# Down stages of an encoder trunk: where the per layer input is loaded, and how the first result is turned

## The chip, the cores and the metric

The kernel runs on one core of a Trainium2 chip. The metric is the device time of one execution in microseconds (us), as the median over runs. The engines are named as the profile names them: PE (TensorE, matrix products; PEld is its loading of stationary operands), DVE (VectorE), ACT (ScalarE), POOL (GpSimd) and SP (SyncE, which here only issues DMAs). Each engine carries out its own instructions in the order in which they were placed in its program; engines wait for one another through semaphores.

## The reference

An encoder trunk of two layers over one sequence of 512 positions with 1024 features, in float32. What matters here:

```python
for i in range(DEPTH):                       # 2 layers
    h = h + 0.5 * swiglu(rmsnorm(h, norm_ffn1[i]), ffn1_w_gate[i], ffn1_w_up[i], ffn1_w_down[i])
    hn = rmsnorm(h, norm_mix[i])
    h = h + (ab_mixer(hn, ...) if i % 2 == 0 else c_mixer(hn, ...))
    h = h + 0.5 * swiglu(rmsnorm(h, norm_ffn2[i]), ffn2_w_gate[i], ffn2_w_up[i], ffn2_w_down[i])
    gate = jax.nn.sigmoid(rmsnorm(h, norm_ple[i]) @ w_ple_gate[i])
    h = h + gate * (p[i] @ w_ple_proj[i])    # p[i]: 512 x 256, the per layer input
return rmsnorm(h, norm_final)

def swiglu(x, w_gate, w_up, w_down):         # 1024 -> 2816 -> 1024
    return (jax.nn.silu(x @ w_gate) * (x @ w_up)) @ w_down
```

There are four `swiglu` in all, two per layer. The product with `w_down` (2816 x 1024) is the down stage that this document is about. The per layer input `p[i]` is used only behind the second `swiglu` of a layer.

## The kernel before

**Arithmetic.** Every float32 operand of a product is split in two: a high part, which ACT rounds (L154), and a low part, the rest, which DVE subtracts (L155, or L218 where a gain is multiplied in). A product is three matmuls: high by high, low by high, high by low. So each weight block costs ACT one pass, DVE one pass, and PE three.

**The down stage** (`down`, L493) computes a 2816 x 1024 by 2816 x 512 product by blocks with seven products instead of eight: weights and inner activations are cut in quarters, and sums of quarters are multiplied ("first" to "seventh"). Each of the seven runs over eleven pairs of inner chunks, cut into six units of 1, 2, 2, 2, 2 and 2 pairs. That makes 42 steps, and their order on PE is a list written by hand (`order`, L604 to L608): step 10 is fifth 2, step 14 is seventh 0, step 17 fifth 4, step 18 seventh 1, step 24 fourth 0, step 28 sixth 3, step 29 seventh 5, and the last ones are third 3, third 4 and third 5 (39 to 41). A step of unit 0 has six matmuls, any other step twelve.

Three things happen around each step (loop at L689): `product` issues its matmuls (L595); `after` (L640) does what is due behind certain steps; `ahead` prepares the operands of the step four further on (`prepare`, L549: splits, sums of weight blocks on DVE at L566, accumulating loads on POOL at L547) and issues the load of the step seven further on (`load`, L529: a wide block through `wide`, L518 and L520, into one of five `wr` buffers, or narrow blocks through `narrow`, L523 and L526, each into one of ten `tmp` buffers). One `wr` buffer serves several products in turn: its weights are split for one product, another quarter is added to it by an accumulating load, and it is split again. It comes free for the next wide load when its last split is done.

**Order.** What passes through `put` (L150) while `pinned` is set keeps its place in the order of the program on its engine. Everything else is placed by a scheduler, by priority and by when it is ready. In the loop `pinned` is set (L680), so the matmuls, splits and weight loads are in fixed order on PE, ACT, DVE, POOL and SP. The loads of the stored `h` (L658) are not pinned.

**The ends of the stage.** The first result is in `c11` and `c21` after fourth 5; its blocks of 128 features are turned back with PE transposes against an identity (`turned`, L614, four per block), added to `h` by DVE (L625) and split for the next phase (`norm_split`, L217 and L218, not pinned). `first_half(m)` does this for block m of 0 to 3; `second_half` does it for two blocks at a time from 4 to 7 (L635), in halves. The transposes write to one of two PSUM banks (`tbank`), which DVE empties. The last part needs the end of third 5 and a subtraction (L696).

**The per layer input.** In the second `swiglu` of a layer `down` gets a function `inner`. Behind step fourth 0 it calls `per_layer` for each of two chunks: a DMA of 256 KB on SP (L481, not pinned) into a `tmp` buffer, and the split of that buffer on ACT and DVE (L154 and L155, pinned).

Of the kernel before, what the change touches and what calls it, by code (L numbers as in the profile page):

```python
# [56 lines left out]
class Trunk:  # L57
# [92 lines left out]
    def put(self, ins):  # L150
        return self.tc.keep_in_program_order(ins) if self.pinned else ins
# [302 lines left out]
    def ffn(self, i, which, k_next):  # L454


        nc, io = self.nc, self.io
        gu, dn = io[f"gu{which}"][i], io[f"dn{which}"][i]
        first = i == 0 and which == 1
        kept = io["xT"].rearrange("p c t -> c p t") if first else self.put_away()  # L460
        a, sums = [], [None] * K2
        rows, t = self.front(gu, first)
        y = self.xg

        def between():
            a.extend(self.turn_back(rows, self.tbank))
            for k in range(READY):
                if 2 * k + 2 <= len(a) and sums[k] is None:
                    sums[k] = self.inner_sums(*a[2 * k:2 * k + 2])

        for j in range(BLOCKS):
            n = 4 * UNIT + j * 8 * UNIT
            rows = self.block(gu[:, n:n + 8 * UNIT], y, t, between, first and j == 0)
        self.begin_norm(k_next)
        p = lambda: [self.per_layer(i, c) for c in range(2)]
        self.down(dn, a, sums, kept, p if which == 2 else None, lambda n: a.extend(self.turn_back(rows, self.tbank, n)))

    def per_layer(self, i, c):

        raw = self.tmp()  # L480
        self.nc.sync.dma_start(raw, self.io["pT"][i, :, c, :])  # L481
        return self.split_chunk(raw, self.nc.vector)

    def inner_sums(self, a, b):

# [7 lines left out]
    def down(self, w, a, sums, kept, inner, turn):  # L493

        nc, H = self.nc, T // 2
# [6 lines left out]
        n = len(units)  # L502
        r1, r2, r3 = [self.bank(), self.bank()], [self.bank(), self.obank()], [self.sbank(), self.sbank()]
        rb = rc = c11 = c5 = c2 = u3 = c21 = None
        x1, x2, x3, x4, raws, more, ops = ({} for _ in range(7))
        put = self.put
# [91 lines left out]
        def copied(p):  # L598
            out = [self.act() for _ in p]
            for o, x in zip(out, p):  # L600
                put(copy(o, x, AF.Copy))
            return out
# [9 lines left out]
        def turned(out, x, j):  # L612
            for i, y in enumerate(x):
                put(nc.tensor.transpose(out[:, i * P:(i + 1) * P], y[:, j * P:(j + 1) * P], self.ident))  # L614

        def floating(f, *x):
            pinned, self.pinned = self.pinned, False
            f(*x)
            self.pinned = pinned

        def first_half(m):
            p, h = self.tbank(), hs[m]
            turned(p[:, l], c11, m)
            turned(p[:, r], c21, m)
            put(nc.vector.scalar_tensor_tensor(h, p, 0.5, h, op0=ALU.mult, op1=ALU.add))  # L625
            self.h[m] = h
            floating(self.norm_split, m)

        def second_half(m, x, c):
            p = self.tbank()  # L630
            for j in range(2):
                turned(p[:, j * H:(j + 1) * H], x, m - M + j)
            for j in range(2):
                h = hs[m + j]
                put(nc.vector.scalar_tensor_tensor(h[:, c], p[:, j * H:(j + 1) * H], 0.5, h[:, c], op0=ALU.mult, op1=ALU.add))  # L635
                self.h[m + j] = h
            for j in range(2):
                floating(self.norm_split, m + j, c)

        def after(kind, s):  # L640
            nonlocal rb, rc, c11, c5, c2, u3, c21
            if (kind, s) in (("first", 2), ("fifth", 1)):
                turn(range(2) if kind == "first" else range(2, 4))
                if kind == "fifth":
                    rb = [self.tbank(), self.tbank()]
            elif (kind, s) == ("first", 5):
                c11 = copied(r1)
                for o, p in zip(c11, r2):
                    put(tt(o, p, o, op=ALU.add))
                rc = [self.bank(), self.obank()]  # L650
            elif (kind, s) == ("fifth", 5):
                c5 = copied(r3)
            elif (kind, s) == ("fourth", 0) and inner:
                self.p = inner()
            elif (kind, s) == ("first", 3):
                hs.extend(self.act() for _ in range(KC))
                for m in range(KC):
                    nc.sync.dma_start(hs[m], kept[m])  # L658
            elif (kind, s) == ("sixth", 5):
                c2, u3 = copied(r1), [self.act(), self.act()]  # L660
                for i in range(2):
                    put(tt(u3[i], c2[i], rb[i], op=sub))
                for i in range(2):
                    put(tt(c5[i], c5[i], u3[i], op=sub))
            elif (kind, s) == ("fourth", 5):
                c21 = [self.act(), self.act()]
                for i in range(2):
                    put(tt(c21[i], rc[i], u3[i], op=ALU.add))
                second_half(M + 2, c5, r)
            elif (kind, s) == ("third", 2):  # L670
                second_half(M, c5, r)
            elif kind == "third" and 2 < s < 5:
                first_half(2 * s - 6)
                first_half(2 * s - 5)

        for i, step in enumerate(order[:LOADS]):
            load(*step)
# [11 lines left out]
        for i, step in enumerate(order):  # L689
            product(*step)  # L690
            after(*step)
            ahead(i + LEAD + 1)
# [941 lines left out]
```

## Time and profile before

| | us |
|---|---|
| runs | 2001.15, 2001.87, 2005.03 |
| median | 2001.87 |
| the profiled execution | 2003.01 |
| its span (first to last instruction) | 2001.2 |

The first and last matmul of the four down stages, as the trace has them:

| stage | layer, swiglu | loads p | L595 from | to | us |
|---|---|---|---|---|---|
| D1 | 0, first | no | 229.1 | 342.3 | 113.2 |
| D2 | 0, second | yes | 857.1 | 975.1 | 118.0 |
| D3 | 1, first | no | 1252.0 | 1364.8 | 112.8 |
| D4 | 1, second | yes | 1815.3 | 1933.3 | 118.0 |

How to read the rows of the profile. A row of the order of time has the start in us from the start of the span, the duration, the engine, the line of the kernel, the operation, "written<-read" by the names of the buffers, the shape, the count if several were merged, and in brackets the idle time of that engine just before with what ended it. A row of the waits is "engine buffer line <- what it waited for: us in total, times, the longest". A row of a stretch has the stretch, its length, then for PE, PEld, DVE, ACT and POOL the busy time and the count, then the granted TensorE clock as a share of full speed, the share of time for which the DMA engines were busy, and the GB/s that they moved. "SPq" is SP's queue of DMA issues; its rows are the issues, and "DMA to landing" is the time from the issue until the data has arrived.

### The profile page before, as it was taken

The page shows a single profiled execution, that of the slowest core. Times are in us where ns is not written, and L with a number is a line of the kernel's source. Part 1 is how long each engine was busy: PE and PEld are TensorE (multiplying, and loading weights), DVE is VectorE, ACT ScalarE, POOL GpSimd, SP SyncE. Part 2 cuts the span into 40 slices and gives each one's busy share as a digit, 9 for nine tenths or more (in the row PEclk, how much of TensorE's full clock was granted, in tenths as well). Part 3 has the DMA queues.
Part 4 walks back from the last instruction along what each step waited for, and adds up shares of the span by engine and source line. Part 5 has one row for each costly group of instructions (what it writes and reads, how often), then busy time and mean ns, then how long its engine had stood idle before and what let it go on. Part 6 is the DMA issues. An engine that isn't in the chain of part 4 may idle for free.

```text
span 2001.2 us, 28069 instructions
## 1 busy us (share of the span) xinstructions
PE 1974.6 (99%) x9702; PEld 1644.8 (82%) x9702; DVE 1551.5 (78%) x2716; ACT 1218.5 (61%) x2107; POOL 334.7 (17%) x390
## 2 busy tenths in 40 slices
PE   9999999999999999999999999999999999999998
PEld 7888887879888888887888888888888888888786
DVE  8787888698767677787786778887888768678785
ACT  7555656477645555565565556655766556657553
POOL 1111111341211212011122120111000122111111
PEclk9999999999999999999999999999999999999999
DMA  9877697543426777779468785894343577768961
GB/s 275 195 200 163 182 232 229 131 96 80 101 64 226 174 179 183 173 213 252 150 219 184 175 193 153 216 247 150 103 133 101 179 189 189 170 147 229 251 194 42
DMA packets 152223, 348.24 MB, mean 174 GB/s; under 512 B 26512, under 2 KB 34192, under 8 KB 152080
## 3 DMA queue, kind: packets, MB, share of 16 engines
q1 hardware_dynamic: 112128, 235.23, 35.4%
q0 software_dynamic: 39808, 111.17, 31.3%
q8 instruction: 76, 1.25, 0.2%
q14 instruction: 67, 0.55, 0.1%
q10 hardware_dynamic: 144, 0.04, 0.0%
HBM read 318.06 MB, written 17.27 MB: 168 GB/s over the span
## 4 chain that ended last, share of the span: by engine, by line
PE 60%; issue 6%; DVE 6%; DMA 5%; ACT 2%; POOL 1%; SPq 0%; DVEq 0%; POOLq 0%; ACTq 0%
PE mm L179 5%; PE mm L181 5%; PE mm L180 5%; PE mm L595 5%; PE mm L369 4%; PE mm L370 4%; PE mm L368 4%; PE sc L595 3%; DMA wr<-in_gu_dram 3%; PE sc L370 2%; PE sc L369 2%; PE sc L368 2%; DVE wl L155 2%; PE ob L595 2%; PE sc L181 1%
## 5 line engine op out<-in xcount | busy, mean ns | idle before, releaser
L154 ACT ACTIVATE wh<-wr 128x1024 fp32r<-128x1024 f32 (+1 forms) x428 | 438.4, 1029 | 412.1 <-PE mm L370 87.3
L155 DVE TENSOR_TENSOR wl<-wr,wh 128x1024 fp32r<-128x1024 f32 (+1 forms) x428 | 509.8, 1195 | 176.5 <-ACT wh L154 168.0
L368 PE MATMUL mm<-wh,act 128*128 128x512 f32 x640 | 251.0, 392 | 0.0
L370 PE MATMUL mm<-wh,act 128*128 128x512 f32 x640 | 250.8, 392 | 0.0
L369 PE MATMUL mm<-wl,act 128*128 128x512 f32 x640 | 249.5, 390 | 0.1
L179 PE MATMUL mm<-act,wh 128*128 128x512 f32 (+1 forms) x472 | 185.0, 394 | 0.4 <-ACT act L154 0.4
L181 PE MATMUL mm<-act,wl 128*128 128x512 f32 (+1 forms) x472 | 184.6, 392 | 0.0
L180 PE MATMUL mm<-act,wh 128*128 128x512 f32 (+1 forms) x472 | 183.9, 390 | 0.0
L154 ACT ACTIVATE wh<-tmp 128x512 fp32r<-128x512 f32 x248 | 144.9, 623 | 63.8 <-PE sc L370 32.7
L595 PE MATMUL mm<-wh,act 128*128 128x512 f32 x528 | 159.5, 397 | 6.3 <-ACT wh L154 6.3
L155 DVE TENSOR_TENSOR wl<-tmp,wh 128x512 fp32r<-128x512 f32 x248 | 160.5, 684 | 2.9 <-ACT wh L154 2.5
L155 DVE TENSOR_TENSOR act<-act,act 128x512 fp32r<-128x512 f32 (+1 forms) x268 | 141.2, 554 | 3.9 <-ACT act L154 3.7
L338 POOL DMA_DIRECT2D wr<-in_gu_dram x80 | 79.5, 996 | 376.9 <-DVE wl L155 373.4
L369 PEld LDWEIGHTS mm<-wl,act 128*128 128x128 f32 x640 | 120.2, 188 | 24.9 <-DVE wl L155 0.7
L370 PEld LDWEIGHTS mm<-wh,act 128*128 128x128 f32 x640 | 120.2, 188 | 24.4
L368 PEld LDWEIGHTS mm<-wh,act 128*128 128x128 f32 x640 | 120.3, 188 | 23.8
L154 ACT ACTIVATE act<-act 128x512 fp32r<-128x512 f32 (+1 forms) x268 | 125.8, 513 | 15.0 <-DVE act L312 8.3
L368 PE MATMUL sc<-wh,act 128*128 128x512 f32 x320 | 124.7, 390 | 0.5 <-DVE act L292 0.5
L370 PE MATMUL sc<-wh,act 128*128 128x512 f32 x320 | 124.7, 390 | 0.0
L369 PE MATMUL sc<-wl,act 128*128 128x512 f32 x320 | 124.6, 389 | 0.0
L595 PEld LDWEIGHTS mm<-wh,act 128*128 128x128 f32 x528 | 100.3, 190 | 27.9 <-ACT wh L154 7.2
L547 POOL DMA_DIRECT2D wr<-in_dn_dram x72 | 62.3, 880 | 358.4 <-DVE wl L155 352.8
(260 smaller groups left out, 4316.3 us busy)
## 6 DMA issues: line engine op xcount, KB each, us to landing
wr<-in_gu_dram SPq DMA_DIRECT2D x92, 512.0 KB, 4.9
tmp<-in_gu_dram SPq DMA_DIRECT2D x160, 256.0 KB, 3.6
wr<-in_gu_dram POOLq DMA_DIRECT2D x80, 512.0 KB, 7.7
tmp<-in_dn_dram SPq DMA_DIRECT2D x132, 256.0 KB, 6.1
wr<-in_dn_dram POOLq DMA_DIRECT2D x60, 512.0 KB, 7.6
tmp<-in_gu_dram POOLq DMA_DIRECT2D x80, 256.0 KB, 6.0
wr<-in_dn_dram SPq DMA_DIRECT2D x40, 512.0 KB, 5.6
act<-kept SPq DMA_DIRECT2D x56, 256.0 KB, 4.6
```

The costliest lines, as they stand in the source:

```text
L154: self.put(self.nc.scalar.activation(hi, src, AF.Copy))
L155: self.put((lo_eng or self.nc.vector).tensor_tensor(lo, src, hi.bitcast(F32), op=ALU.subtract))
L179: mm(out, stat[0], mov[0], start=start, stop=False)
L180: mm(out, stat[0], mov[1], start=False, stop=False)
L181: return mm(out, stat[1], mov[0], start=False, stop=stop)
L338: nc.gpsimd.dma_start(raw, q[:, u * UNIT:(u + 1) * UNIT], accum_op=ALU.add)
L368: mm(p, xh, wh, start=start and k == 0, stop=False, skip_group_check=True)
L369: mm(p, xh, wl, start=False, stop=False, skip_group_check=True)
L370: self.last_mm = mm(p, xl, wh, start=False, stop=stop and k == half - 1, skip_group_check=True)
L547: put(nc.gpsimd.dma_start(raw, b[:, u.start * T:u.stop * T], accum_op=ALU.add))
L595: put(nc.tensor.matmul(p, x[k][a][:, c], w[b][:, j * T:(j + 1) * T], start=start and k == a == b == 0, stop=stop and b == 1 and k == u.sto ...
```

## The change

Two edits in `down`, and one in what calls it.

The per layer input: its two DMAs are issued behind step fifth 2, pinned, and its splits stand behind step seventh 0; before, both stood behind fourth 0, with the DMAs not pinned. `inner` is now a function that gives the source of a chunk, and `per_layer` is gone.

The turning of the first result: before, behind third 3 blocks 0 and 1, behind third 4 blocks 2 and 3. Now behind third 3 block 0, behind third 4 blocks 1 and 2, behind third 5 block 3. This holds for all four down stages.

```diff
-        p = lambda: [self.per_layer(i, c) for c in range(2)]
-        self.down(dn, a, sums, kept, p if which == 2 else None, lambda n: a.extend(self.turn_back(rows, self.tbank, n)))
-
-    def per_layer(self, i, c):
-
-        raw = self.tmp()
-        self.nc.sync.dma_start(raw, self.io["pT"][i, :, c, :])
-        return self.split_chunk(raw, self.nc.vector)
+        inner = lambda c: io["pT"][i, :, c, :]
+        self.down(dn, a, sums, kept, inner if which == 2 else None, lambda n: a.extend(self.turn_back(rows, self.tbank, n)))
...
-            elif (kind, s) == ("fourth", 0) and inner:
-                self.p = inner()
+            elif (kind, s) == ("fifth", 2) and inner:
+                for c in range(2):
+                    more["inner", c] = self.tmp()
+                    put(nc.sync.dma_start(more["inner", c], inner(c)))
+            elif (kind, s) == ("seventh", 0) and inner:
+                self.p = [self.split_chunk(more.pop(("inner", c)), nc.vector) for c in range(2)]
...
-            elif kind == "third" and 2 < s < 5:
-                first_half(2 * s - 6)
-                first_half(2 * s - 5)
+            elif kind == "third" and s > 2:
+                for m in ((0,), (1, 2), (3,))[s - 3]:
+                    first_half(m)
```

## The prediction

> **What bounds the kernel now.** I read the page's busy shares first, then who TensorE (PE) and ScalarE (ACT) wait for.
>
> ```profile
> span 2001.2 us, 28069 instructions
> PE 1974.6 (99%) x9702; PEld 1644.8 (82%) x9702; DVE 1551.5 (78%) x2716; ACT 1218.5 (61%) x2107; POOL 334.7 (17%) x390
> ...
> PE mm L595 <- ACT wh L154: 6.3, 2, 3.3
> ...
> ACT act L154 <- DMA tmp<-in_pT_dram: 11.4, 4, 3.8
> ```
>
> PE is busy 99% of the span, so only what makes PE wait or run slowly can be gained. Its longest wait is at the products of the down stages (L595): two waits, 6.3 us together, both for the high half of a weight block. In ACT's list four waits for the per layer input p (L481) hold 11.4 us. I number the down stages D1 to D4 in order of time; p is loaded in D2 and D4. The order of time on PE, ACT and the SP queue shows that the two waits are one event per stage.
>
> ```profile
> 915.61 0.97 SPq L481 DMA_DIRECT2D tmp<-in_pT_dram  x2
> ...
> 925.66 0.63 ACT L154 ACTIVATE act<-tmp 128x512 fp32r<-128x512 f32 x1 [3.04 <-DMA tmp<-in_pT_dram]
> 928.86 0.63 ACT L154 ACTIVATE act<-tmp 128x512 fp32r<-128x512 f32 x1 [2.57 <-DMA tmp<-in_pT_dram]
> 929.39 1.04 ACT L154 ACTIVATE wh<-wr 128x1024 fp32r<-128x1024 f32 x1
> ...
> 926.76 0.39 PE L595 MATMUL ob<-wl,act 128*128 128x512 f32 x1
> 930.49 2.75 PE L595 MATMUL mm<-wh,act 128*128 128x512 f32 x8 [3.34 <-ACT wh L154]
> ...
> 938.46 0.39 PE L595 MATMUL mm<-wh,act 128*128 128x512 f32 x1
> ...
> 1884.92 0.39 PE L595 MATMUL ob<-wl,act 128*128 128x512 f32 x1
> 1888.32 3.78 PE L595 MATMUL mm<-wh,act 128*128 128x512 f32 x8 [3.00 <-ACT wh L154]
> ...
> 1896.67 0.39 PE L595 MATMUL mm<-wh,act 128*128 128x512 f32 x1
> ```
>
> In D2 the two loads of p are issued at 915.6 and arrive at 925.7 and 928.9. The splits of p stand in ACT's fixed order ahead of the weight block of sixth 3, so that block is split at 929.4, and PE, out of work since 926.8, starts at 930.5.
>
> How much is lost needs the pace of an undisturbed product: D1, which loads no p, has the same steps (sixth 3, then seventh 5).
>
> ```profile
> 298.97 1.98 PE L595 MATMUL mm<-wh,act 128*128 128x512 f32 x8
> ...
> 301.69 1.77 PE L595 MATMUL tr<-wh,act 128*128 128x512 f32 x6
> 303.67 0.73 PE L595 MATMUL tr<-wh,act 128*128 128x512 f32 x2 [0.20 <-DVE act L155]
> ...
> 305.16 0.39 PE L595 MATMUL mm<-wh,act 128*128 128x512 f32 x1
> ...
> 1324.59 2.36 PE L595 MATMUL tr<-wh,act 128*128 128x512 f32 x8
> ...
> 1327.72 0.40 PE L595 MATMUL mm<-wh,act 128*128 128x512 f32 x1
> ```
>
> Twelve matmuls take 301.69 - 298.97 = 2.72 us, 0.227 each. In D2 the two products after the matmul at 926.76 should end at 926.99 + 5.44 = 932.43; the next product starts at 938.46. **Lost: 6.03 us in D2**, and likewise 1896.67 - (1885.15 + 5.44) = **6.08 us in D4**: 12.1 us. Only 6.3 of it is waiting. The rest is a slower clock:
>
> ```profile
> 931.80:934.70 2.90, 2.90 (x8) 1.95 (x7) 1.64 (x3) 1.63 (x3) 0.86 (x1) 0.50 1.00 343
> 1888.30:1894.10 5.80, 5.78 (x14) 4.53 (x15) 4.54 (x7) 3.20 (x6) 1.46 (x2) 0.50 1.07 372
> ```
>
> The column behind POOL is the granted clock: 0.50 for 2.9 us in D2 and 5.8 us in D4, after PE had stood idle.
>
> **Part 1, the loads of p.** Their issue moves from behind fourth 0 (step 24) to behind fifth 2 (step 10), now in fixed order on SP; the splits (two on ACT, two on VectorE, DVE) from step 24 to behind seventh 0 (step 14). Nothing is added or removed. *Will p be there in time?* On SP it now stands behind the wide load of first 5:
>
> ```profile
> 871.07 6.03 SPq L520 DMA_DIRECT2D wr<-in_dn_dram  x2
> ...
> DMA to landing us min/median/max: 10.4/10.4/10.4
> ...
> 872.00:887.00 15.00, 15.00 (x76) 12.55 (x75) 12.97 (x23) 10.00 (x18) 1.73 (x2) 1.00 0.99 290
> 887.00:907.00 20.00, 20.00 (x90) 16.58 (x89) 16.03 (x24) 11.02 (x16) 4.35 (x5) 1.00 0.77 184
> ```
>
> The landing row is of the load at 871.1 alone: it lands at 881.5. p's 0.52 MB at 290 GB/s are 1.8 us more, so p lands near 883.5. Queued behind p on SP is seventh 1's load, issued at 877 and taken by L566 only at 895.3 (row below): 1.8 us of delay are covered by some ten. The DMA engines are full to 887, then 77% busy for 20 us (4.6 us free), which absorbs p. Two of the ten tmp buffers and four of the 64 act buffers are held earlier; the narrow loads that come next have about as much slack. All this: nothing. Without that cover p's 1.8 us would pass to PE twice, 3.6 us.
>
> *What do the splits push?*
>
> ```profile
> 894.18 1.22 DVE L155 TENSOR_TENSOR wl<-wr,wh 128x1024 fp32r<-128x1024 f32 x1
> 895.32 1.29 DVE L566 TENSOR_TENSOR wr<-wr,tmp 128x512 f32<-128x512 f32 x2
> ...
> 896.77 1.58 ACT L154 ACTIVATE wh<-wr 128x1024 fp32r<-128x1024 f32 x2 [3.39 <-DVE wr L566]
> ...
> 900.39 0.69 DVE L649 TENSOR_TENSOR act<-mm,act 128x512 f32<-128x512 f32 x1 [0.69 <-ACT act L601]
> ...
> 906.44 0.33 SPq L520 DMA_DIRECT2D wr<-in_dn_dram  x1
> ...
> 917.47 0.69 DVE L566 TENSOR_TENSOR wr<-wr,tmp 128x512 f32<-128x512 f32 x1 [1.35 <-DMA tmp<-in_dn_dram]
> ...
> 1857.23 1.83 DVE L155 TENSOR_TENSOR wl<-wr,wh 128x1024 fp32r<-128x1024 f32 x2 [1.26 <-ACT wh L154]
> 1858.97 0.68 DVE L649 TENSOR_TENSOR act<-mm,act 128x512 f32<-128x512 f32 x1
> ```
>
> The new place is between 894.2 and 895.3 on DVE. ACT's two copies fall into its 3.39 us of idling: free. DVE's two subtractions (0.69 each by itself, 1.2 for both as a pair overlaps) push L566, ACT's block behind it at 896.8, and all that follows in order. In D2 DVE's wait of 0.69 at 900.4 for ACT's copy of the finished first result, whose time PE sets, swallows 0.7 of it. About 0.5 us reach the split of fifth 5; that split frees the buffer that SP waits for at 906.4, so the 0.5 passes to seventh 4's narrow load, which DVE awaits at 917.5. In D4 DVE goes from 1857.2 into L649 without a wait, and I pass on the whole 1.2. From seventh 4 on DVE has little slack before the products of D1's rows above, where PE already loses 305.16 - 301.69 - 2.72 = 0.75 us (and 1327.72 - 1324.59 - 2.72 = 0.41 in D3). So the loss that is left there is 0.75 + 0.5 = 1.25 us in D2 and 0.41 + 1.2 = 1.6 in D4, 2.85 together. Its bounds: nothing at all, if PE's lead there is larger than in D1 and D3; or the whole 1.2 in D2 too, 3.6. **Part 1: -12.1 + 2.85 = -9.3 us** (bounds -12.1 and -8.5).
>
> [...] As my remaining waits are well under 3 us, they should cost themselves alone.
>
> **Part 2, the turning.** Per stage the first result's four groups of four transposes (L614), each with its DVE update (L625) and split (L217, L218), move from two and two behind third 3 and third 4 to one, two and one behind third 3, 4 and 5. The count stays.
>
> ```profile
> PE tr L614 <- DVE act L635: 0.7, 2, 0.4
> ...
> 332.94 0.63 PE L614 MATMUL tr<-ident,act 128*128 128x128 f32 x4 [0.37 <-DVE act L635]
> ...
> 336.52 0.66 PE L614 MATMUL tr<-ident,act 128*128 128x128 f32 x4 [0.18 <-DVE act L625]
> ...
> 972.16 0.60 PE L614 MATMUL tr<-ident,act 128*128 128x128 f32 x4
> ...
> 973.28 0.68 DVE L625 SCALAR_TENSOR_TENSOR act<-tr,act 128x512 f32<-128x512 f32 x1
> ...
> 975.43 0.68 DVE L625 SCALAR_TENSOR_TENSOR act<-tr,act 128x512 f32<-128x512 f32 x1
> ```
>
> In D1 the second group behind third 3 waits 0.37 us for its bank, which DVE has yet to empty; one product later that bank is free. PE's list has two such waits in the whole run, 0.7 us together (the other is at the same place of D3); I take both away: -0.7. The wait of 0.18 behind third 4 stays, since the second group there needs the bank of the first. D2 and D4 show no such wait: nothing. Is the last group late? Its transposes run at 972.2, its update only at 975.4: DVE supplies one column block every 2.15 us, and PE is 3 us ahead. Transposes behind the last product, which then starts sooner, cost nothing as long as the next phase's matmuls fill PE. Bounds: -1.1 (the two waits of 0.18 go too) to +2 (a wait of 0.5 in each stage, more than any of these rows shows). **Part 2: -0.7.**
>
> **Sum.** The profiled execution took 2003.01 us (span 2001.2 and 1.8 around it), 1.1 above the median of the three runs, 2001.87. -9.3 - 0.7 = -10.0: 1993.0 for it, **1991.9** as a median. Its own range by the bounds: -13.2 to -6.5, 1988.7 to 1995.4 as a median.
>
> **The rivals.** *A new wait takes the old one's place:* p's splits push the chain to seventh 4's load by more than 1.2 us, as load and split wait for each other, and PE waits about 3 us in D2 and D4. For it: 917.5 waits for that load already. Against it: p's bytes no longer share the DMA engines from 915.6 on, when half of that load is still on its way. That is 2.7 us more than summed per stage, a gain of about 4.5: 1997. *The load does not come early:* SP or ACT waits for p at the new place, and the stall moves to step 18. Against it: ten us between landing and use. Gain 0 to 2: 2001. *Slower:* the last group behind third 5 starves PE at all four ends: the next phase needs blocks 0 to 3 first, and if PE runs through its other work before block 3 is split, it idles over 3 us and drops to half clock, at the 6 us an event that D2 shows. 4 x 6 - 9.3 = +14.7: 2016.5. It decides when DVE delivers block 3 later than 3 us after PE's last ready matmul; against it stands that DVE's pace there, not PE's place, sets block 3.
>
> **How the numbers follow.** Forecast 0.76, new wait 0.13, not early 0.06, slower 0.05. A measurement tells 0.2%, 4 us, from no change: faster (below 1997.9) 0.88, same 0.07, slower 0.05. The range takes the forecast's own, 1 us below it for work that falls into another order, and the new wait: 1987.5 to 1997.5.
>
> **What would show it.** Right: no waiting of ACT for in_pT; its two loads of D2 issued near 872 and split with DVE between fifth 4's low half and L566 of seventh 1; granted clock 1.00 throughout D2 and D4; each about 5 us shorter; in D1 one wait for L635 fewer. Wrong: a wait of PE over 1.5 us for wh or act of seventh 4 to fourth 2; a gap of PE behind third 5; SP's loads behind p waiting for tmp buffers.

## The result, and the profile after

| | before | after |
|---|---|---|
| runs beside each other on one chip | 6, median 2000.87 us (1998.11 to 2005.03) | 6, median 1991.91 us (1991.00 to 1992.47) |
| the profiled execution | 2003.01 | 1991.14 |
| its span | 2001.2 | 1989.3 |

The ratio after to before is 0.995, with a 95% interval of 0.9939 to 0.996; it stands for -10.0 us, while the two medians differ by 9.0. The forecast was 1991.9 us, from a median of before of 2001.87. That it meets the measured median to 0.1 us is luck. Two further series of the changed kernel, each beside the kernel before on one chip, gave ratios of 0.9949 and 0.9936.

**The page and PE's waits.** Two fences: the first lines of the page of the kernel after, and one row of the view of what PE waited for (engine, tile, line, what released it: us in total, times, the longest).

```profile
span 1989.3 us, 28060 instructions
PE 1966.7 (99%) x9702; PEld 1641.4 (83%) x9702; DVE 1550.9 (78%) x2716; ACT 1218.4 (61%) x2107; POOL 334.5 (17%) x390
```

```profile
PE tr L608 <- DVE act L619: 2.8, 4, 0.8
```

The work is the same, but PE is busy 7.9 us less (1974.6 before). In the trace of before PE is busy for 3.4 us of D2 and 6.0 us of D4 at a clock of 0.50. There twelve matmuls took 5.28 us (D4, 1888.32 to 1893.60) where undisturbed ones take 2.72, so by estimate 9.4 x (1 - 2.72 / 5.28) = 4.6 us of it goes with that clock. The rest I could not place. The two waits for `wh`, 6.3 us, are gone from PE's list, and so are the two for L635 and two for L218 at the same ends (`PE ob L180 <- DVE act L218: 0.6, 2, 0.3` in before's list). In their place stand four waits for L619 (L625 before), one at the end of each down stage. Together they hold 2.8 us, and the prediction had 0.2 at each of two.

**The place of the stall.** The order of time on PE in D2, from the last matmul of the product ahead of step 28 (sixth 3) to the first of step 30. Columns: start, duration, instruction, and in brackets the idle time before it.

```profile
926.30 0.39 PE L589 MATMUL ob<-wl,act 128*128 128x512 f32 x1
926.53 1.98 PE L589 MATMUL mm<-wh,act 128*128 128x512 f32 x8
...
929.25 2.06 PE L589 MATMUL tr<-wh,act 128*128 128x512 f32 x8
...
932.08 0.39 PE L589 MATMUL mm<-wh,act 128*128 128x512 f32 x1
```

Nothing stands in brackets. The two products take 932.08 - 926.53 = 5.55 us, against the 5.44 of undisturbed ones: 0.11 us is lost where it had been 6.03. The windows over the whole of D2 and D4, from the first matmul to the last, give the clock (columns: window, length, busy PE, PEld, DVE, ACT, POOL, then granted clock, DMA share, GB/s); first D2 and D4 after, then D2 before.

```profile
856.70:966.90 110.20, 109.42 (x500) 90.28 (x499) 95.25 (x156) 72.28 (x124) 15.85 (x19) 1.00 0.83 225
1808.50:1918.70 110.20, 109.41 (x500) 90.25 (x499) 95.22 (x156) 72.14 (x124) 15.85 (x19) 1.00 0.84 225
```

```profile
857.10:975.50 118.40, 114.84 (x515) 93.68 (x514) 98.45 (x160) 74.31 (x127) 16.40 (x20) 0.99 0.81 219
```

The clock is 1.00 throughout. The window of D2 is 8.2 us shorter, but only 5.9 of it is the stall. The rest is mostly order: in the kernel before, the last product ran among matmuls of the next phase, so 515 matmuls lie in that window and 500 in this one.

**The loads and splits of p at their new place**, from the order of time on SP, ACT and DVE in D2; behind it the time from issue to landing of the two loads of D2.

```profile
870.52 3.60 SPq L650 DMA_DIRECT2D tmp<-in_pT_dram  x2
876.38 0.33 SPq L514 DMA_DIRECT2D wr<-in_dn_dram  x1
...
892.84 1.14 ACT L154 ACTIVATE act<-tmp 128x512 fp32r<-128x512 f32 x2
...
894.86 1.28 DVE L155 TENSOR_TENSOR act<-tmp,act 128x512 fp32r<-128x512 f32 x2
896.06 1.28 DVE L560 TENSOR_TENSOR wr<-wr,tmp 128x512 f32<-128x512 f32 x2
```

```profile
DMA to landing us min/median/max: 8.3/9.6/11.0
```

The loads are issued at 870.5 and 873.8 and land by 882.1, which is 25.4 us into the stage; the forecast 883.5 was 26.4 us into its own. They are split from 892.8 on without a wait, so ten us of cover are left. The wide load queued behind them on SP is issued 19.7 us into the stage, and 19.6 before.

**The ends.** The order of time on PE behind third 4 and third 5 of D1 and D2, and on DVE ahead of the wait in D1.

```profile
334.61 0.60 PE L608 MATMUL tr<-ident,act 128*128 128x128 f32 x4
335.78 0.66 PE L608 MATMUL tr<-ident,act 128*128 128x128 f32 x4 [0.57 <-DVE act L619]
...
963.58 0.66 PE L608 MATMUL tr<-ident,act 128*128 128x128 f32 x4 [0.78 <-DVE act L619]
...
966.83 0.60 PE L608 MATMUL tr<-ident,act 128*128 128x128 f32 x4
967.19 0.47 PE L179 MATMUL mm<-act,wh 128*128 128x512 f32 x1
...
331.98 1.22 DVE L155 TENSOR_TENSOR wl<-wr,wh 128x1024 fp32r<-128x1024 f32 x1
...
333.51 1.22 DVE L155 TENSOR_TENSOR wl<-wr,wh 128x1024 fp32r<-128x1024 f32 x1
...
335.04 0.68 DVE L619 SCALAR_TENSOR_TENSOR act<-tr,act 128x512 f32<-128x512 f32 x1
```

The second group behind third 4 waits for the bank of block 0. That block was transposed by 332.0, but DVE comes to it only at 335.04, because two splits of weights for the next phase stand ahead of it. Behind third 5 there is no gap: 966.83 and 0.36 us later the next phase.

**Where the 11.9 us between the two spans lie.** I measure two stretches of each stage. The *loss* is the time from the stage's first matmul to the first of step 30, less the 75.29 us (69.85 + 5.44) of an undisturbed one. The *end* is the time from the start of third 3 to the 150th matmul behind it; the same 150 are in it whatever the kernel, in another order.

| us | loss D1, D2, D3, D4 | end D1, D2, D3, D4 |
|---|---|---|
| before | 0.75, 6.04, 0.41, 6.08 | 28.92, 30.92, 28.84, 30.91 |
| after | 0.00, 0.11, 0.56, 0.22 | 27.83, 31.76, 27.90, 31.66 |
| difference | -0.75, -5.93, +0.15, -5.86 | -1.09, +0.84, -0.94, +0.75 |

Their sum is -12.8, of which 0.9 is given back elsewhere in the run. The ends of D1 and D3 gain more than was forecast, and those of D2 and D4 become longer, which was not forecast at all. How much of this is the change, and how much one execution against another, was for the experiments.

### The profile page after: what moved, and what is told of

It is laid out like the page before. It is cut to its first block, busy times and chain, and to the rows that moved or that the text cites. A ratio compares the mean times of both kernels' runs of the same rounds, so it can differ in the third digit from the quotient of the medians.

```text
span 1989.3 us, 28060 instructions
## 1 busy us (share of the span) xinstructions
PE 1966.7 (99%) x9702; PEld 1641.4 (83%) x9702; DVE 1550.9 (78%) x2716; ACT 1218.4 (61%) x2107; POOL 334.5 (17%) x390
## 4 chain that ended last, share of the span: by engine, by line
PE 88%; DVE 5%; issue 2%; DMA 2%; ACT 2%; SPq 0%; POOL 0%; DVEq 0%; ACTq 0%; POOLq 0%
PE mm L589 8%; PE mm L369 7%; PE mm L368 7%; PE mm L370 7%; PE sc L589 6%; PE mm L179 5%; PE mm L181 5%; PE mm L180 5%; PE sc L368 3%; PE sc L370 3%; PE sc L369 3%; PE ob L589 3%; PE tr L589 3%; PE tr L449 2%; PE ob L368 2%
## 5 line engine op out<-in xcount | busy, mean ns | idle before, releaser
L155 DVE TENSOR_TENSOR wl<-wr,wh 128x1024 fp32r<-128x1024 f32 (+1 forms) x428 | 509.7, 1194 | 187.5 <-ACT wh L154 178.1
L180 PE MATMUL mm<-act,wh 128*128 128x512 f32 (+1 forms) x472 | 184.4, 391 | 0.0
L154 ACT ACTIVATE wh<-tmp 128x512 fp32r<-128x512 f32 x248 | 144.6, 623 | 62.5 <-PE sc L370 32.7
L155 DVE TENSOR_TENSOR wl<-tmp,wh 128x512 fp32r<-128x512 f32 x248 | 160.2, 682 | 3.0 <-ACT wh L154 2.6
L155 DVE TENSOR_TENSOR act<-act,act 128x512 fp32r<-128x512 f32 (+1 forms) x268 | 140.8, 552 | 3.8 <-ACT act L154 3.7
L541 POOL DMA_DIRECT2D wr<-in_dn_dram x72 | 62.3, 880 | 349.1 <-DVE wl L155 349.1
```

The costliest lines, as they stand in the source:

```text
L154: self.put(self.nc.scalar.activation(hi, src, AF.Copy))
L155: self.put((lo_eng or self.nc.vector).tensor_tensor(lo, src, hi.bitcast(F32), op=ALU.subtract))
L180: mm(out, stat[0], mov[1], start=False, stop=False)
L541: put(nc.gpsimd.dma_start(raw, b[:, u.start * T:u.stop * T], accum_op=ALU.add))
```

## The experiments

All series, with the sums of loss and end over the stages without p (D1, D3) and with it (D2, D4), from the one profiled execution of each:

| kernel | median us (runs) | ratio to before, 95% | loss D1+D3 | loss D2+D4 | end D1+D3 | end D2+D4 |
|---|---|---|---|---|---|---|
| before | 2000.87 (6) | | 1.16 | 12.12 | 57.76 | 61.83 |
| before_again | 2003.88 (1) | | 1.90 | 11.78 | 57.63 | 61.84 |
| turn_only | 1999.43 (11) | 0.9987 [0.9978, 0.9996] | 1.57 | 10.08 | 55.91 | 61.38 |
| p_only | 1994.75 (5) | 0.9957 [0.9945, 0.997] | 0.47 | 1.15 | 57.25 | 63.60 |
| dma_early | 1996.11 (5) | 0.9963 [0.9949, 0.9976] | 0.02 | 2.34 | 57.53 | 63.75 |
| p_before_s4 | 1998.16 (8) | 0.9977 [0.9966, 0.9987] | 1.71 | 4.34 | 57.03 | 63.32 |
| after | 1991.91 (6) | 0.995 [0.9939, 0.996] | 0.56 | 0.33 | 55.72 | 63.42 |
| after_again | 1993.4 (5) | 0.9949 [0.9936, 0.9961] | 1.18 | 2.36 | 56.09 | 63.56 |
| turn_bank | 1992.7 (5) | 0.9948 [0.9936, 0.9961] | 1.55 | 0.98 | 55.75 | 63.00 |
| turn_112 | 1991.68 (5) | 0.9943 [0.9929, 0.9956] | 0.33 | 1.87 | 54.99 | 62.55 |
| after_third | 1989.56 (5) | 0.9936 [0.9922, 0.9949] | 0.52 | 0.29 | 55.79 | 63.17 |
| turn_112_again | 1988.98 (5) | 0.9936 [0.9924, 0.9949] | 0.01 | 0.00 | 54.65 | 62.71 |
| soon_112 | 1988.51 (5) | 0.9935 [0.9922, 0.9947] | 0.01 | 2.11 | 55.16 | 62.54 |

before_again to p_before_s4 ran in one set, except that p_before_s4 stood with after_again, turn_112 and turn_bank; the last three lines are a third set. Medians of before in these sets: 2002.16, 2003.07 and 2002.93. Only ratios are compared across sets.

### before_again: the kernel before, once more

No edit; one run.

> The kernel before, profiled once more, with nothing changed. Theory: the two waits of PE for the block of sixth 3 are there again, about 3 us each, but the stretch at half clock behind them has another length (2.9 and 5.8 us in the first trace), so the loss in D2 and D4 together differs from 12.1 us by up to 3; the span lies between 1996 and 2003. Rival: the loss is fixed by the program; it is 12.1 us again within 0.5, and the spread of the runs of before (1998.1 to 2005.0) comes from elsewhere. Either way the loss at sixth 3 and seventh 5 of D1 and D3, which load no p, was 0.75 and 0.41 us; after the change 0 and 0.62. If it moves again by as much, D1's gain is not the change's doing.

The loss in D2 and D4 is 6.29 and 5.48 us, 11.8 together against 12.1: it belongs to the kernel, not to one execution, as the rival of the expectation had it. D1 now loses 0.06 and D3 1.84, where the first trace had 0.75 and 0.41. These two stages load no p, so **losses of 0 to 1.9 us come and go there by themselves**. The stall of D4 in PE's order of time:

```profile
1889.56 3.60 PE L595 MATMUL mm<-wh,act 128*128 128x512 f32 x8 [2.84 <-ACT wh L154]
```

After a wait of 2.84 us the eight matmuls take 3.60 us where undisturbed ones took 1.98: half clock, as in the first trace. Here the clock was at 0.50 for 3.41 us in each stage. In the first trace that was 3.4 us in D2 and 6.8 in D4 (1887.47 to 1894.29; the 2.9 and 5.8 us of the prediction are only the lengths of its windows). The loss is nearly the same all the same; turn_only, below, shows why.

### p_only: the loads of p early, the turning as before

The changed kernel with the old grouping:

```diff
-            elif kind == "third" and s > 2:
-                for m in ((0,), (1, 2), (3,))[s - 3]:
-                    first_half(m)
+            elif kind == "third" and 2 < s < 5:
+                first_half(2 * s - 6)
+                first_half(2 * s - 5)
```

> The per layer input as after the change, the turning as before. Theory (all of the gain is the stall of p and the clock behind it): 1991.5 us, the same as after within 1 us; D2 and D4 each 5 to 6 us shorter than before; no wait of PE for the update of block 0 (L619 of after), but the small waits of before at D1's and D3's ends are back. Rival (as the prediction had it, the turning gives 0.7): 1992.6.

The ratio 0.9957 of 2002.16 is -8.6 us (interval -11.0 to -6.0). Both expected times, 1991.5 and 1992.6, lie below the median of 1994.75; the interval overlaps with that of the changed kernel (0.995), so the two series alone don't tell what the turning adds. The losses in D2 and D4 are 0.06 and 1.09, about 10.6 less than before_again. The ends of the same two stages became 1.8 us longer together. Here is D2, on PE and on DVE, first with p early, then in the kernel before.

```profile
959.54 2.10 PE L589 MATMUL sc<-wh,act 128*128 128x512 f32 x8
...
963.63 0.63 PE L608 MATMUL tr<-ident,act 128*128 128x128 f32 x4 [0.42 <-DVE act L629]
...
967.20 0.66 PE L608 MATMUL tr<-ident,act 128*128 128x128 f32 x4 [0.20 <-DVE act L619]
...
962.74 0.74 DVE L629 SCALAR_TENSOR_TENSOR act<-tr,act 128x256 f32<-128x256 f32 x2
```

```profile
962.42 2.10 PE L595 MATMUL sc<-wh,act 128*128 128x512 f32 x8
...
965.27 1.03 PE L614 MATMUL tr<-ident,act 128*128 128x128 f32 x8
...
963.84 0.74 DVE L635 SCALAR_TENSOR_TENSOR act<-tr,act 128x256 f32<-128x256 f32 x2
```

Measured from the start of third 3 (959.54 and 962.42), DVE's update that frees the bank comes at 3.20 us with p early and at 1.42 us before. In the kernel before, the stall had let DVE run 1.8 us ahead of PE, and the transposes (x8) passed without a wait. **With the stall gone DVE has no such lead, and the two waits of D1, for L635 and for L625, appear in D2 and D4 as well** (L629 and L619 in this kernel): in D4 the update comes at 3.05 us, and in before's D1 at 2.93. All kernels with p early have ends of 62.5 to 63.8 us in D2 and D4, those with p late 61.4 to 61.8; for the old turning 63.56 against 61.84, so 1.7 us are given back. The idle time of PE there, 0.00 before and 0.62 and 0.60 here, is 1.2 of them.

### turn_only: the new turning alone

```diff
-            elif kind == "third" and 2 < s < 5:
-                first_half(2 * s - 6)
-                first_half(2 * s - 5)
+            elif kind == "third" and s > 2:
+                for m in ((0,), (1, 2), (3,))[s - 3]:
+                    first_half(m)
```

> The turning as after the change, the per layer input as before. Theory (the turning exchanges the waits behind third 3 for one behind third 4 in each of four stages, 2.8 us of waiting in the trace of after): 0 to +0.5 us against before, thus 2001 us, with both stalls of about 3 us still there. Rival (the prediction): -0.7 us against before, 2000.2.

The ratio 0.9987 is -2.6 us (interval -4.4 to -0.8), a larger gain than either expectation had (+0.5 to 0, and -0.7). The ends of D1 and D3 are 0.8 to 0.9 us shorter each than in before_again, those of D2 and D4 0.2 each. In PE's list of waits the two for L635 and the two for L218 are gone and longer ones stand behind third 4:

```profile
PE tr L614 <- DVE act L625: 1.4, 2, 0.8
```

Idle time explains only a small part of the gain in D1: it fell from 0.92 us in before to 0.77 here and 0.57 in after. The rest lies in many short steps between matmuls, and I could not trace it to one row. Of D1's gain about half is lost again later in the same phase: to the 700th matmul behind third 3 the old turning took 134.5 to 135.1 us in five traces, the new one 134.0 to 134.7 in four. In D3 the whole gain stays (117.7 to 117.9 against 116.9 to 117.2). With p early the ends of D2 and D4 are 0.2 us shorter together (63.38 against 63.56, means of three traces each). So the turning is worth about 0.5 + 0.8 + 0.2 = 1.5 us by the traces, inside the interval of the series.

**This execution also shows what the stall is made of.** In its D4, p landed 2.0 us earlier in the stage than in the kernel before (69.4 against 71.4 us behind the first matmul). PE and ACT of that D4, in order of time:

```profile
1886.34 2.11 PE L595 MATMUL mm<-wh,act 128*128 128x512 f32 x8 [1.02 <-ACT wh L154]
...
1890.55 2.07 PE L595 MATMUL tr<-wh,act 128*128 128x512 f32 x6 [1.19 <-ACT act L154]
...
1894.32 0.39 PE L595 MATMUL mm<-wh,act 128*128 128x512 f32 x1
...
1885.24 1.04 ACT L154 ACTIVATE wh<-wr 128x1024 fp32r<-128x1024 f32 x1
1888.91 1.06 ACT L154 ACTIVATE wh<-wr 128x1024 fp32r<-128x1024 f32 x1 [2.63 <-DVE wr L566]
```

And the same places of its D2, where p landed late:

```profile
930.60 3.63 PE L595 MATMUL mm<-wh,act 128*128 128x512 f32 x8 [3.72 <-ACT wh L154]
...
938.58 0.39 PE L595 MATMUL mm<-wh,act 128*128 128x512 f32 x1
...
929.51 1.04 ACT L154 ACTIVATE wh<-wr 128x1024 fp32r<-128x1024 f32 x1
933.18 1.06 ACT L154 ACTIVATE wh<-wr 128x1024 fp32r<-128x1024 f32 x1 [2.63 <-DVE wr L566]
```

The windows from the stall on, first of D2, then of D4:

```profile
930.60:934.30 3.70, 3.70 (x9) 2.93 (x10) 2.44 (x4) 1.12 (x2) 0.86 (x1) 0.54 1.05 347
1885.20:1894.30 9.10, 6.60 (x25) 4.30 (x25) 7.41 (x12) 6.47 (x12) 1.73 (x2) 1.00 1.05 350
```

In D4 PE waited only 1.0 us and the clock stayed at 1.00; in D2 it waited 3.7 us and ran at half clock. Yet from the start of sixth 3 to step 30 both took **7.98 us** (1894.32 - 1886.34 and 938.58 - 930.60). What sets that time is ACT and DVE: the block of seventh 5 is split 3.67 us behind that of sixth 3 in both, since the subtraction for sixth 3 (L155, 1.2 us) and the sum L566 (1.3) must pass on DVE in between. At full clock PE waits for what ACT and DVE do behind that split (1.19 us for the copy of activations that follows it on ACT at 1889.88, and 0.20); at half clock it spends the same time in slow matmuls. So the 2.54 us that a stall costs beyond its first wait (7.98 - 5.44) are not the clock's doing. Of the six stalls in three traces five took 7.97 to 7.99 us for these two steps. Only D4 of before took 8.35, and there alone the half clock lasted 6.8 us instead of 3.4; by this its price is 0.4 us in one stall of six. That is one stall at full clock against five, so it rests on a single execution.

### dma_early and p_before_s4: early loads, late splits

Both keep the old turning. The first issues the loads behind fifth 2, like the change, but leaves the splits behind fourth 0, where they were. The second moves its loads as well, to behind sixth 0 (895.8 in its D2), some ten us ahead of seventh 4's narrow loads (905.9).

```diff
-            elif (kind, s) == ("seventh", 0) and inner:
+            elif (kind, s) == ("fourth", 0) and inner:
                 self.p = [self.split_chunk(more.pop(("inner", c)), nc.vector) for c in range(2)]
```

```diff
-            elif (kind, s) == ("fifth", 2) and inner:
+            elif (kind, s) == ("sixth", 0) and inner:
```

> The loads of p behind fifth 2 as after the change, but their splits behind fourth 0 and the turning as before. Theory (the loads' time is what counts; the place of the splits only has to lie behind their landing): 1992 us, no wait of ACT for p, within 1 us of p with early splits. Rival (the splits at the late place take ACT and DVE time just where DVE has no slack, so that seventh 5 and fourth 2 wait): PE loses 1 to 1.5 us in D2 and D4 each at steps 28 to 30, 1994.5 us.

> The loads of p behind sixth 0 (step 19), so that SP issues them just ahead of seventh 4's load; the splits behind fourth 0 and the turning as before. Theory (the prediction's chain: a delay of seventh 4's load passes to PE one to one): p's 1.8 us come on top of what the kernel with early loads and late splits loses at steps 28 and 29 (1.1 and 1.2 us): PE loses about 3 us in D2 and in D4, 1999.5 us in all, perhaps with ACT waiting for p. Rival (the time that seventh 4's load takes to land varies by 1 us or more by itself, and the lead takes up the rest): within 1 us of early loads with late splits, 1996.

dma_early loses 1.10 us in D2 and 1.24 in D4, where p_only loses 0.06 and 1.09. DVE's order of time in D2 shows what the late splits push, first in dma_early, then in the kernel after.

```profile
925.27 1.28 DVE L155 TENSOR_TENSOR act<-tmp,act 128x512 fp32r<-128x512 f32 x2
926.48 1.21 DVE L155 TENSOR_TENSOR wl<-wr,wh 128x1024 fp32r<-128x1024 f32 x1
927.61 1.28 DVE L560 TENSOR_TENSOR wr<-wr,tmp 128x512 f32<-128x512 f32 x2
```

```profile
925.22 1.29 DVE L560 TENSOR_TENSOR wr<-wr,tmp 128x512 f32<-128x512 f32 x2
```

The sum of seventh 5's weights (L560) starts 927.61 - 858.08 = 69.53 us into the stage in dma_early and 925.22 - 856.68 = 68.54 in after. The 0.99 us between them is almost the 1.10 lost in that D2. So in D2 the place of the splits is worth about 1 us by the traces, as the rival of the expectation had it. D4 doesn't tell: p_only lost as much there, and in both kernels another load landed late in it (see soon_112). The two series overlap (0.9963 and 0.9957), so the times do not show it either.

p_before_s4 may be slower than p_only (the intervals overlap) and loses 1.40 and 2.94. Its ratio 0.9977 is -4.7 us, between the two expectations. The collision it was made for did not take place: its four loads of p landed within 5.5 us, before seventh 4's loads were issued, and DVE's sum for seventh 4 does not wait for a load.

```profile
DMA to landing us min/median/max: 4.9/5.2/5.5
```

```profile
915.66 1.28 DVE L560 TENSOR_TENSOR wr<-wr,tmp 128x512 f32<-128x512 f32 x2
```

In D2 about 1.1 us is the late splits, as in dma_early. In D4 another load adds to it. The accumulating load that POOL issues right behind p's loads, 42.3 and 43.3 us into D2 and D4, took 6.9 and 7.4 us to land, against 5.7 in D1 and D3 of the same trace; in D4 ACT waits 2.71 us for it at 1863.24, and 0.63 at the same place of dma_early. So p's loads probably do collide, though not with seventh 4's. It isn't shown: the same load took 7.6 us in two stages without p (D1 of after_again and of turn_bank).

### after_again and after_third: the changed kernel, two more series

No edit.

> The changed kernel as it is, beside the others of this set. Its ratio to the kernel before was 0.995; expected 0.995 again. Theory (the gain is a stall of 3 us per stage with half clock behind it, in D2 and D4): its runs lie within 2 us of one another, while those of before spread over 4 us or more. Its trace should show again one wait of 0.6 to 0.8 us for L619 behind third 4 in each of the four stages.

> The changed kernel once more, beside the others of this set: ratio 0.994 to 0.996; remaining loss in steps 28 and 29 of D2 and D4 together between 0.3 and 2.4 us, as in its two traces so far.

The losses in D2 and D4 are 0.35 and 2.01, then 0.36 and 0: what is left at steps 28 and 29 varies from one execution to the next, as in D1 and D3. The three ends of each stage agree within 0.25 us. The waits for L619 are there again, and the ratio 0.9949 is the expected one; 0.9936 lies just outside the expected range. The runs of after_again spread over 3.2 us and those of before beside them over 2.7, so the forecast that the change narrows the spread did not come true in that set.

### turn_bank, turn_112 and turn_112_again: the wait for L619 taken away in two ways

turn_bank gives block 2 a bank of another pool, so that it needn't wait for that of block 0; turn_112 moves block 2 behind third 5, to groups of one, one and two.

```diff
-            p, h = self.tbank(), hs[m]
+            p, h = self.bank() if m == 2 else self.tbank(), hs[m]
```

```diff
-                for m in ((0,), (1, 2), (3,))[s - 3]:
+                for m in ((0,), (1,), (2, 3))[s - 3]:
```

> As after the change, but block 2 of the first result is turned into a bank of the group that the first result has left, so that its transposes do not wait for block 0's update. Theory: the wait for L619 behind third 4 is gone in all four stages, 2 to 3 us less than after, about 1989.5 where after has 1992. Rival (DVE's pace): the same as after within 1 us, PE waits as long a few us later.

> As after the change, but the blocks of the first result behind third 3, 4 and 5 in groups of one, one and two. Theory (the 2.8 us of waiting for L619 behind third 4 are PE time that comes back when nothing needs that bank there): 2 to 3 us less than after, about 1989.5 where after has 1992. Rival (DVE delivers one block of the next phase's operands every 2.15 us whatever PE does, so a wait taken away ahead of third 5 comes back behind it): the same as after within 1 us, with the wait for L619 now behind third 5 or at the first matmuls of the next phase.

> The changed kernel with the groups of transposes as one, one and two; a second series, to tell it from the changed kernel. Theory (the wait of 0.6 to 0.8 us of PE for L619 behind third 4 is a cost of the group of two in the middle): no such wait in any of the four stages, each end (start of third 3 to the 150th matmul behind it) 0.4 to 0.6 us shorter than in the changed kernel, 1 to 2.5 us less in all, ratio near 0.9940. Rival (what is won at the ends is lost again in the next phases, whose splits then come later): median within 0.5 us of the changed kernel's.

Both take the waits for L619 away. turn_bank gets short ones for another line in return, the first fence (PE's list of waits). turn_112 gets none: in its D1, the second fence (PE's order of time), third 5 follows one group after third 4, and the group of two (x8) behind it passes unhindered.

```profile
PE tr L608 <- DVE act L694: 0.8, 4, 0.2
```

```profile
334.56 0.60 PE L608 MATMUL tr<-ident,act 128*128 128x128 f32 x4
334.92 2.09 PE L589 MATMUL sc<-wh,act 128*128 128x512 f32 x8
...
337.76 1.06 PE L608 MATMUL tr<-ident,act 128*128 128x128 f32 x8
338.57 0.47 PE L179 MATMUL ob<-act,wh 128*128 128x512 f32 x1
```

turn_bank is 0.7 us below the changed kernel's median in its set, as its rival had it (within 1 us), though the wait that comes instead holds 0.8 us and not 2.8. The four ends are 1.7 us shorter with turn_112's grouping than in the changed kernel (117.5 against 119.2, three traces each). The medians lie 1.7 us below the changed kernel's in one set and 0.6 in the other, each within the spread of either; the ratios are 0.9943 against 0.9949, and 0.9936 against 0.9936. It removes the wait and may be a little faster; the times don't settle it.

### soon_112: the splits of p three steps earlier still

turn_112, and:

```diff
-            elif (kind, s) == ("seventh", 0) and inner:
+            elif (kind, s) == ("second", 4) and inner:
```

> As one, one and two, and p's splits three steps earlier still (behind second 4, near 886 us instead of 894 in D2). Theory (what is left at steps 28 and 29 comes from how late the narrow loads land, which varies by itself, and not from p's splits): between 0 and 2.5 us left there in D2 and D4 together, as with the splits behind seventh 0; median within 1 us of the same kernel with the later splits. Rival, the prediction's own step (each 0.1 us by which the splits push DVE reaches seventh 4's load): with splits that have eight more us to be absorbed, nothing is left in either stage, and the median is 1 to 2 us lower.

D2 loses nothing, but D4 loses 2.11 us. The kernel with the later splits lost nothing in either stage in one trace, and 0.24 and 1.62 in the other. The median is 0.5 us lower, within the spread. More room for the splits thus removes nothing that can be seen.

The traces show where the loss in D4 comes from. POOL issues an accumulating load (L541 here, L547 before) 8.95 us behind the first matmul of every stage, ahead of p's loads; it lands between 17.2 and 19.6 us. ACT's wait for it in D4, first of after_again, then of after:

```profile
1828.92 1.06 ACT L154 ACTIVATE wh<-wr 128x1024 fp32r<-128x1024 f32 x1 [2.97 <-DMA wr<-in_dn_dram]
```

```profile
1825.99 1.06 ACT L154 ACTIVATE wh<-wr 128x1024 fp32r<-128x1024 f32 x1 [0.81 <-DMA wr<-in_dn_dram]
```

Of the eight traces with early loads and early splits, the four in whose D4 it landed at 18.5 us or later (p_only, after_again, turn_112, soon_112) lost 1.1 to 2.1 us there; the four in which it landed at 17.4 to 17.8 us lost 0.4 at most. The delay is there before p's splits begin, so **what remains in D4 is not passed on from them**. Nor do p's early loads cause it: with p late, in before and before_again, it landed at 18.7 and 18.6 us in D4 as well. It isn't the narrow loads of the expectation either: in soon_112's D4 DVE waits for none of them. Why the accumulating load lands late in some executions stays open.

## Why the prediction was right, and where its terms were not

**The total held, and its main cause is shown.** p's late load, with the half clock behind the stall, cost 12.1, 11.8 and 10.1 us in the three traces that have it, 11.3 on the mean; the forecast had 12.1. Once p is loaded early it is gone in all ten such traces. ACT doesn't wait for p, the loads were issued and landed about a us from the times given, they hold up no queue, and the clock is 1.00 in D2 and D4. *Not early*, *new wait* and *slower* all fall: there is no wait of ACT for p, none of PE of 1.5 us at the products of D2 and D4 in the changed kernel, and no gap behind third 5.

The size of three more terms was off, and the errors cancelled.

**1. What is left at steps 28 and 29 was put too high.** The prediction argued that p's splits push DVE by 1.2 us, that "about 0.5 us reach the split of fifth 5", that this passes through the freed buffer to seventh 4's narrow load, and that it adds to D1's and D3's own losses: 2.85. The eight traces with early loads and early splits lost 0.33, 2.36, 0.29, 0.98, 1.87, 0.00, 1.15 and 2.11: 1.1 on the mean. Two steps failed. The losses of D1 and D3 (0.75 and 0.41) were taken for a constant base, and they vary from 0 to 1.8 us between single executions. And the push of the splits does not pass through seventh 4's load to PE, as its landing doesn't follow its issue. These rows give the time from issue to landing of seventh 4's two narrow loads in D2, first after, then before (issued at 906.8 and 907.3 in both):

```profile
DMA to landing us min/median/max: 6.4/7.6/8.9
```

```profile
DMA to landing us min/median/max: 7.8/9.0/10.1
```

The last of them was issued 0.4 us later in its stage than before, just as the chain had it (50.6 against 50.2 us behind the first matmul), and yet landed 0.8 us earlier. DVE had waited 1.35 us for it before and comes to this sum without a wait after: that wait took up the push. In D4 the issue stands at 50.6 us in both, but there the stage of before was already late, since its accumulating load landed at 18.7 us and that of after at 17.4. Of the 1.1 us that are left, 0.9 are in D4 and go with that load (soon_112).

**2. "D2 and D4 show no such wait: nothing"** was true of the trace of before only because of the stall: it had given DVE its lead of 1.8 us. With the stall taken away the two stages wait as D1 and D3 do. That gives back 1.7 us (61.84 to 63.56 with the old turning). The prediction asked what is late next at the products and not at the ends of the same stages.

**3. The turning is worth more than 0.7**: 2.6 us by the series (0.8 to 4.4), about 1.5 by the traces. The prediction counted the two named waits alone. It left out the two for L218, 0.6 us together, that go with them. It also held that the wait of 0.18 behind third 4 would stay as it was; it grew to between 0.6 and 0.8 in all four stages, as DVE has two weight splits ahead of block 0's update. Most of what outweighs this lies in short steps that I could not trace.

Put together with the measured sizes: -11.3 + 1.1 + 1.7 - 1.5 = -10.0, against the forecast's -12.1 + 2.85 - 0.7 = -10.0. The three measured ratios give -10.0, -10.2 and -12.8 us. The total came out right through two errors in each direction, which is luck; what the prediction got on its own merits is the stall.

**4. "The rest is a slower clock" was the wrong cause of a right size.** The forecast took the 12.1 us as 6.3 of waiting and the rest half clock. The rows of turn_only show the same 7.98 us for the two steps at full clock: behind the first wait, seventh 5's block is 3.67 us behind sixth 3's on ACT and DVE, and the half clock runs within that time. The sum didn't suffer, since it took the whole loss as measured and the change removes its first cause. For the same reason "my remaining waits are well under 3 us, they should cost themselves alone" doesn't hold: a wait of 1.0 us at sixth 3 was followed by 2.5 us more at the next step.

At the two steps the runs measured -11.3 + 1.1 = -10.2, against -9.3 in part 1, and the chain on ACT and DVE, not the clock, fills the time behind the wait. The half clock lasted 3.41 us in four of the five stalls where it occurred, and 6.8 in D4 of before. There the clock dropped at 1887.47, 2.2 us after the end of PE's last matmul and 0.85 before the next; in before_again a wait of 2.84 us was followed by it as well.

## What to carry to other kernels

A stall in one place gives the engines that don't stall a lead (1.8 us to DVE here), and their places further on look free because of it: before a stall is removed, compare the stretch behind it with the same stretch of a stage that has none, and put that stage's waits on the bill. A low clock behind a stall need not be its price (7.98 us for two products at 0.50 and at 1.00 here): look first whether the operands would have been there any sooner. Take the base of such a comparison from several executions or stages, as a single trace shows losses that come and go: here 0 to 1.9 us in D1 and D3, and in D4 0.4 us at most or 1.1 to 2.1, with the landing of one load. Move a load and what consumes it together: the early load removed the stall, but in the one stage that tells, with its consumers left in the old place the DVE still came about a us late to the next block.

## What the runs showed of the hardware that was not expected

- **The same load lands 1 to 2 us earlier or later from one execution to the next.** The accumulating load that POOL issues 8.95 us into each stage landed at 17.4 us in two D4 and at 19.6 in two others. Such a delay is handed on: p's second load of D4 was issued at 59.9 us and landed at 71.4 in the kernel before, and in turn_only, where the accumulating load had come 1.1 us sooner, it was issued at 59.0 and landed at 69.4. The stall cost 3.7 us there and 5.5 to 6.4 in the other five.
- **The clock was at 0.50 behind waits of 2.84 us and more, and stayed at 1.00 behind waits of 1.2 us at the same products.** The five stalls with waits of 2.84 to 3.72 us show the one, the stall with waits of 1.0 and 1.2 us the other; between these the products of the down stages show nothing. Elsewhere the length of the wait alone does not tell. In the trace of after a wait of 1.46 us (at 35.60) passed at a clock of 1.00, and near its end the clock was at 0.50 from 1981.02 on, where the longest wait just before was 1.56 us (at 1979.69). In p_only it was at 0.50 from 535.66 to 539.07, behind 24 matmuls of small operands (64x128 and 128x16) and no wait of PE; in after the same 24 (531.22 to 534.26) passed at 1.00.
- **Half clock for 3 us can cost nothing.** Five stalls took 7.97 to 7.99 us for two products, four of them behind a drop to half clock and one at a clock of 1.00, as the operands came at that pace.
